# Transposing blocks by DMA in 16-bit halves instead of by TensorE, in a decoder layer

## The chip, the cores and the metric

The kernel runs on one core of a Trainium2 chip. TensorE (PE) multiplies matrices and writes PSUM; VectorE (DVE) and ScalarE (ACT) do elementwise work; GpSimd (POOL) does a little elementwise work and issues some DMAs; SyncE (SP) issues most DMAs. The metric is the device time of one launch in microseconds. The kernel before takes 2216.7 us (median of 3 runs, 2216.55 to 2218.02).

## The reference, cut to what matters

One decoder layer in float32 over 256 tokens of width 2048: a SwiGLU feed-forward, a mixer of two parallel branches (windowed attention and RWKV-7), a cross-attention into 256 memory tokens, a second SwiGLU, a final norm. The part around the change is the end of the mixer and the start of the cross-attention:

```python
merged = gate_attn * (y_attn @ w_proj_attn) + gate_rwkv * (y_rwkv @ w_proj_rwkv)
x = x + merged @ w_out
# cross-attention
h = rms_norm(x, norm_g)                  # the third norm
mn = rms_norm(mem, mem_norm_g)
q = (h @ w_q).reshape(B, T, CROSS_HEADS, CROSS_HEAD_DIM)
km, vm = jnp.split(mn @ w_kv, 2, axis=-1)
```

## The kernel before

**Products.** Every weight product runs on PE in a split form of float32. A weight tile of two 128-row chunks by 512 columns (512 KB, one *unit*) is loaded by SP into a tile `raw`. ACT casts it to `hi` (L370), DVE forms `lo = raw - hi` (L371), and PE does three matmuls for each chunk and each half of the tokens: hi·hi, lo·hi, hi·lo (L447 to L449). The left operand is the activation, turned so that features lie on the partitions, and split into hi and lo in the same way. A product with w_proj_rwkv has 4 units for a block of 512 columns, one with w_out 8. Units are prepared ahead of their use: `next_item` loads four units ahead and casts two ahead, with four `raw` buffers and three `hi` and three `lo` buffers.

**Background work.** Everything else is written as generators in named groups of an `Interleave`. After each half of a unit (six matmuls) `bg.tick()` takes one step of the first generators of each group (as many as the group's limit). `later_by(n, steps)` and `idle(n)` let n ticks go by. This gives the order in which the program is written. A planner then puts the instructions of each engine in an order by the times that it expects, so that work whose data is expected early may stand ahead of its written place; a tile's slot is given when it becomes free, and its first writer waits for the slot's last user. `tc.issue_after` pins an instruction behind another.

**The stage around the change.** After the RWKV branch (`yr`) is ready, four products with w_proj_rwkv give the four column blocks n of the merged branches: DVE multiplies by the gate (L1595), POOL adds the attention branch (L1596) into `m`, a tile of 128 partitions, 2 token halves and 512 columns. `merged(m, n)` waits four ticks, lets PE transpose the block in eight 128 x 128 pieces (`feat`, L639: two PSUM banks of four pieces), and `split` (L644, L645) writes the hi part (ACT) and the lo part (DVE) into `mt`. Four products with w_out follow, which read `mt`: two of a product's eight units for each block n. After each, DVE adds the residual block (L1618) into `x2`, and `n3.block` transposes that block in eight pieces on PE, multiplies by the gain into hi (ACT, L695) and lo (DVE, L696), and sums the squares (ACT, L707). `n3.x` is read two products later, by w_cross_q. Between them runs the first product with w_cross_kv, whose left side is the memory. The memory's blocks (`memory`, L1602 to L1609) arrive already turned (`memt`) and need no transposes; its gain products stand on the same lines L695 and L696 as `mehi` and `melo`.

**Buffers.** The mixer's larger temporaries are tiles named by `t4`, 4 KB on each partition, which share 23 slots (N4). In this stage `mt` holds eight, the memory's hi and lo eight, `x2` up to four, and `mem` with `memt` two for the block in work.

**Queues.** SP's queue carries the weight loads and the memory's loads; POOL's queue carries the residual's reloads (L1615) and those of the gates. A load waits on SP for its `raw` buffer, that is for the `lo` of the unit four before it.

Of the kernel before, what the change touches and what calls it, by code (L numbers as in the profile page):

```python
# [6 lines left out]

F32 = mybir.dt.float32
F32R = mybir.dt.float32r
AF = mybir.ActivationFunctionType  # L10
ALU = mybir.AluOpType
AX = mybir.AxisListType
# [3 lines left out]
P = 128  # L16
# [120 lines left out]
def decoder_layer(ctx: ExitStack, tc: tile.TileContext, a: dict, out: bass.AP):  # L137
    nc = tc.nc
    act, dve, pool, pe = nc.scalar, nc.vector, nc.gpsimd, nc.tensor
# [7 lines left out]
    bg = Interleave()  # L147
# [5 lines left out]
    bg.group("norm", 1)  # L153
    bg.group("mem", 1)
    bg.group("stage", 4)

    def f32(x):
        return x.bitcast(F32)
# [14 lines left out]
    def idle(n):  # L173
        for _ in range(n):
            yield

    def later_by(n, steps):
        yield from idle(n)
        yield from steps
# [19 lines left out]
    def mixer_constants(sp):  # L199
# [31 lines left out]
        for v in (bdones, bdmean):  # L231
            r = sp.tile([P, P], F32R, name="ones_r" + str(len(ones_r)))
            act.copy(r[:], v[:])
# [36 lines left out]
    for entry in weight_plan(a):  # L270
# [4 lines left out]
        w, k0, nk, c0, n = entry  # L275
# [5 lines left out]
        for k in range(k0, k0 + nk, 2 * KU):  # L281
            u = len(units)
            units += [(v, k + i, c, 512) for v, c in zip(w, c0) for i in (0, KU)]
            for i in range(2):
                q = (k - k0) // KU + i
# [79 lines left out]
    def split_unit(u, rows=slice(0, KU)):  # L365
        n, raw = units[u][3], raws[u]
        hi = wp.tile([P, KU, n], F32R, tag="hi", name="hi")
        lo = wp.tile([P, KU, n], F32R, tag="lo", name="lo")
        for s in (slice(0, 1), slice(1, 2)) if u < AHEAD else (rows,):
# [4 lines left out]
    def two_parts(v, e):  # L374
        sp = at["pool"]
        hi = sp.tile([P, KU, 512], F32R, tag="thi" + e, name="thi")
        lo = sp.tile([P, KU, 512], F32R, tag="tlo" + e, name="tlo")
        act.copy(hi[:], v[:])  # L378
# [46 lines left out]
    def product(x: Act, w, skew=False, bank=acc):  # L425

        pw, _, nk, _, n = plan[at["product"]]
        assert pw.tensor is w.tensor
        at["product"] += 1
        o = [bank() for _ in range(2)]  # L430
        skewed = range(nk - AHEAD * KU - KU, nk, KU) if skew else range(nk, nk)
        for k in range(0, nk - KU * len(skewed), KU):
            bg.until(lambda: all(k + i in x.done for i in range(KU)))
            u = next_item()
            for t in range(2):
                multiply(o[t][:, :n], x, u, k, t, nk)
                bg.tick()
        last = [(k, next_item()) for k in skewed]
        for t in range(2):
            for k, u in last:  # L440
                multiply(o[t][:, :n], x, u, k, t, nk)
        return o
# [16 lines left out]
    def combinations(sp, x: Act, seven, name, ready=lambda: True, early=True, n=0):  # L459
# [4 lines left out]
        n = n or sum(4 if q in seven else 2 for q in pairs)  # L464
        parts = [sp.tile([P, n, P], F32R, tag=name + e, name=name + e) for e in ("hi", "lo")]
        c = {"parts": parts, "at": {}, "done": False, "seven": seven, "early": early}
# [40 lines left out]
    def product_pair(x: Act, c, w, first, middle, out, onto=()):  # L507
# [12 lines left out]
        for to, there in onto:  # L520
            b[to] = rings[to]()
            act.activation(b[to][:], there, AF.Copy, scale=2.0)
            begun.add(to)
# [56 lines left out]
    def gate_and_up(sp, x: Act, c, r, w):  # L580
# [14 lines left out]
        def out(b, to):  # L595
            t = int(to in ("p4", "p5"))
            if to in ("p2", "p4"):
                dve.tensor_tensor(hb[:, t], b[to][:], u3[:] if t else hb[:, 0], ALU.add)
                act.activation(hb[:, t], hb[:, t], AF.Silu, scale=r[t])
            else:  # L600
# [7 lines left out]
    def down(h: Act, c, w, xs):  # L608
# [6 lines left out]
        def first(b):  # L615
            act.activation(x00, b["p1"][:], AF.Copy, scale=0.5)

# [14 lines left out]
    def feat(tok, cols):  # L632


        b = tr()
        for i, col in enumerate(cols):
            for t in range(2):
                o = (2 * i + t) * P
                pe.transpose(b[:, o : o + P], tok[:, t, col : col + P], ident[:])  # L639
        return b[:].rearrange("p (c t) -> p c t", c=2)  # L640

    def split(x: Act, c, n, src):

        act.copy(x.at(0, c, n), src)  # L644
        dve.tensor_tensor(x.at(1, c, n), src, f32(x.at(0, c, n)), ALU.subtract)  # L645
        x.done |= set(range(c, c + n))


    class Norm:
# [9 lines left out]
        def begin(self, turned):  # L659
# [13 lines left out]
            begun = dve.tensor_tensor(lo[:, 0], raw[:, 0], f32(hi[:, 0]), ALU.subtract)  # L673
            act.activation(x.at(0, 1), turned[:, 1], AF.Copy, scale=g[1])
            with tc.issue_after(begun.ins):
# [7 lines left out]
        def features(self, n, src=None, turned=None):  # L683
# [5 lines left out]
            for h, b in enumerate(banks):  # L689
                for j in range(2):  # L690
# [3 lines left out]
                    g = self.gain[:, c : c + 1]  # L694
                    self.last = act.activation(self.x.at(0, c), b[:, j, :], AF.Copy, scale=g)  # L695
                    dve.scalar_tensor_tensor(  # L696
# [6 lines left out]
        def squares(self, n, src):  # L703

            with tc.issue_after(self.last.ins):
                for t in range(2):
                    act.activation(  # L707
                        junk_t[:], src[:, t, :], AF.Square, accum_out=self.ss[:, t, n : n + 1]
                    )
# [94 lines left out]
    def blk(d, n):  # L804
        return d[:, n * 512 : (n + 1) * 512].rearrange("(t p) n -> p t n", p=P)
# [14 lines left out]
    with tc.tile_pool(name="f1", bufs=1, reuse_waits="tile") as sp:  # L820
# [8 lines left out]
        turned = f32(sp.tile([P, KD, T], F32R, tag="hlo", name="hlo")[:])  # L829
# [52 lines left out]
    with tc.tile_pool(name="mx", bufs=1, reuse_waits="tile") as sp:  # L882
# [3 lines left out]
        def t4(name, shape=(P, 4, T), dt=F32):  # L886
            return sp.tile(list(shape), dt, tag="t4", name=name, bufs=N4)
# [4 lines left out]
        def act_tiles(name, n):  # L892
            return Act(
                [t4(name + "hi", dt=F32R) for _ in range(n)],
                [t4(name + "lo", dt=F32R) for _ in range(n)], 4,
            )
# [6 lines left out]

        C4 = [0, P, 2 * P, 3 * P]

        def halves_of(v, hi, lo):
            act.copy(hi, v)
            dve.tensor_tensor(lo, v, f32(hi), ALU.subtract)
            return hi, lo
# [670 lines left out]
        mt = act_tiles("mt", 4)  # L1580

        def merged(m, n):
            yield from idle(4)
            banks = [feat(m, C4[q : q + 2]) for q in (0, 2)]
            for q, b in zip((0, 2), banks):
                split(mt, 4 * n + q, 2, b)
                yield

        for n in range(4):
            g, m = t4("gl", (P, 2, 512)), t4("ml", (P, 2, 512))  # L1590
            pool.dma_start(g[:], blk(grd, n))
            pool.dma_start(m[:], blk(md, n))
            pr = product(yr, W["w_proj_rwkv"])
            for t in range(2):
                dve.tensor_tensor(g[:, t, :], pr[t][:], g[:, t, :], ALU.mult)  # L1595
                pool.tensor_tensor(m[:, t, :], g[:, t, :], m[:, t, :], ALU.add)  # L1596
            bg.spawn("feat", merged(m, n))

        n3 = Norm(g_cross)
        nm_ = Norm(g_mem, act_tiles("me", 4))  # L1600
# [11 lines left out]
        for n in range(4):  # L1612
            s = t4("x2", (P, 2, 512))
            x2.append(s)
            pool.dma_start(s[:], blk(x1d, n))  # L1615
            po = product(mt, W["w_out"])
            for t in range(2):
                dve.tensor_tensor(s[:, t, :], po[t][:], s[:, t, :], ALU.add)  # L1618
            bg.spawn("feat", later_by(2, n3.block(n, s)))
            if n == 0:  # L1620
                bg.spawn("mem", memory())

# [72 lines left out]
    with tc.tile_pool(name="f2", bufs=1, reuse_waits="tile") as sp:  # L1695
# [51 lines left out]
        for t in range(2):  # L1747
            m, r = (stat.tile([P, 1], F32, tag=e, name=e) for e in ("ms", "rs"))
# [72 lines left out]
```

## Time and profile before

| what | value |
|---|---|
| median of the runs | 2216.7 us |
| the profiled execution | 2216.82 us, of which 2215.1 us are its span |
| PE busy | 2200.8 us, 99% of the span |
| DVE, ACT, POOL busy | 1802.6, 1275.5, 106.9 us |
| PE clock granted | 0.999 |
| from HBM | 440.49 MB read, 23.59 MB written |

Products with w_proj_rwkv run from about 1267 to 1314 us of the span, those with w_out from there to about 1405 us. The page gives busy times over the whole span, a strip of 40 slices, the DMA queues, the chain of waits that ended last, and groups of instructions by line. The trace also answers for single tiles, lines and windows of time.

### The profile page before, as it was taken

The numbers are of one execution on the slowest core, as the hardware profiler recorded it, in microseconds if no ns is written. First come the engines' busy times: TensorE is split into PE (matmuls) and PEld (weight loads), VectorE is DVE, ScalarE is ACT, GpSimd is POOL, SyncE is SP. The second block draws the span as 40 slices with busy tenths as digits, with TensorE's granted clock in tenths as the row PEclk, the third lists the DMA queues.
The fourth block names the chain that finished last, engine by engine and source line by source line (L and its number), as shares of the span: only waits on it lengthen the run. The fifth ranks groups of instructions, "written<-read, shape, count | busy, mean of one in ns | idle before, by whom it ended". The sixth has DMA issues, their size and how long they took to land.

```text
span 2215.1 us, 28167 instructions
## 1 busy us (share of the span) xinstructions
PE 2200.8 (99%) x10520; PEld 1816.7 (82%) x10520; DVE 1802.6 (81%) x2316; ACT 1275.5 (58%) x1677; POOL 106.9 (5%) x184
## 2 busy tenths in 40 slices
PE   9999999999999999999999999999999999999998
PEld 7888888888888878888888888888888888888886
DVE  7998888998989476877667666558999899998996
ACT  7555555555556477644544546556565565655654
POOL 0000000000000001000321030001000000000000
PEclk9999999999999999999999999999999999999999
DMA  8555555565556545677778687558665666666573
GB/s 306 194 206 192 206 195 203 195 204 193 197 192 211 174 132 164 212 225 215 224 220 290 206 272 269 185 165 275 221 221 189 207 233 208 217 205 210 200 244 136
DMA packets 198280, 466.02 MB, mean 210 GB/s; under 512 B 15520, under 2 KB 17920, under 8 KB 187136
## 3 DMA queue, kind: packets, MB, share of 16 engines
q1 hardware_dynamic: 188976, 438.08, 59.2%
q0 software_dynamic: 7648, 23.52, 3.5%
q10 hardware_dynamic: 1520, 2.63, 0.3%
q8 instruction: 82, 1.34, 0.3%
q14 instruction: 54, 0.44, 0.1%
HBM read 440.49 MB, written 23.59 MB: 210 GB/s over the span
## 4 chain that ended last, share of the span: by engine, by line
PE 93%; DVE 3%; DMA 2%; ACT 1%; issue 1%; SPq 0%; POOLq 0%; POOL 0%; DVEq 0%; ACTq 0%
PE acc L447 19%; PE acc L448 19%; PE acc L449 19%; PE mm L447 8%; PE mm L448 8%; PE mm L449 8%; PE tr L639 2%; PE tr L448 2%; PE tr L447 2%; PE tr L449 2%; DMA raw<-in_ffn_w_up_dram 1%; DVE lo L371 1%; PE mm L1441 1%; DVE tlo L379 1%; PE tr L1371 0%
## 5 line engine op out<-in xcount | busy, mean ns | idle before, releaser
L370 ACT CAST hi<-raw 128x1024 fp32r<-128x1024 f32 (+1 forms) x768 | 754.6, 993 | 671.8 <-PE acc L449 483.1
L371 DVE TENSOR_TENSOR lo<-raw,hi 128x1024 fp32r<-128x1024 f32 (+1 forms) x768 | 879.4, 1149 | 314.9 <-ACT hi L370 312.4
L447 PE MATMUL acc<-hi,xhi 128*128 128x512 f32 (+1 forms) x1134 | 445.4, 394 | 1.9 <-ACT hi L672 1.1
L448 PE MATMUL acc<-lo,xhi 128*128 128x512 f32 (+1 forms) x1134 | 440.0, 388 | 1.6 <-DVE lo L371 1.5
L449 PE MATMUL acc<-hi,xlo 128*128 128x512 f32 (+1 forms) x1134 | 439.5, 388 | 0.0
L447 PEld LDWEIGHTS acc<-hi,xhi 128*128 128x128 f32 x1134 | 212.9, 188 | 47.4 <-issue 3.2
L448 PEld LDWEIGHTS acc<-lo,xhi 128*128 128x128 f32 x1134 | 213.0, 188 | 44.4 <-DVE lo L371 3.1
L449 PEld LDWEIGHTS acc<-hi,xlo 128*128 128x128 f32 x1134 | 212.9, 188 | 43.4 <-issue 0.4
L378 ACT CAST thi<-raw 128x1024 fp32r<-128x1024 f32 x192 | 199.9, 1051 | 64.8 <-DVE raw L401 44.4
L379 DVE TENSOR_TENSOR tlo<-raw,thi 128x1024 fp32r<-128x1024 f32 x192 | 232.3, 1218 | 0.9 <-ACT thi L378 0.3
L447 PE MATMUL mm<-hi,xhi 128*128 128x512 f32 x402 | 156.6, 389 | 0.0
L448 PE MATMUL mm<-lo,xhi 128*128 128x512 f32 x402 | 156.5, 389 | 0.0
L449 PE MATMUL mm<-hi,xlo 128*128 128x512 f32 x402 | 156.4, 389 | 0.0
L448 PE MATMUL acc<-lo,hhi 128*128 128x512 f32 x372 | 145.3, 391 | 0.0
L449 PE MATMUL acc<-hi,hlo 128*128 128x512 f32 x372 | 145.3, 391 | 0.0
L447 PE MATMUL acc<-hi,hhi 128*128 128x512 f32 x372 | 145.0, 390 | 0.0
L447 PEld LDWEIGHTS mm<-hi,xhi 128*128 128x128 f32 x402 | 75.5, 188 | 16.2 <-ACT hi L370 0.5
L448 PEld LDWEIGHTS mm<-lo,xhi 128*128 128x128 f32 x402 | 75.5, 188 | 15.8
L449 PEld LDWEIGHTS mm<-hi,xlo 128*128 128x128 f32 x402 | 75.5, 188 | 15.6
L448 PEld LDWEIGHTS acc<-lo,hhi 128*128 128x128 f32 x372 | 69.8, 188 | 14.4
L447 PEld LDWEIGHTS acc<-hi,hhi 128*128 128x128 f32 x372 | 69.9, 188 | 14.3
L449 PEld LDWEIGHTS acc<-hi,hlo 128*128 128x128 f32 x372 | 69.9, 188 | 14.0
(441 smaller groups left out, 3527.4 us busy)
## 6 DMA issues: line engine op xcount, KB each, us to landing
raw<-in_ffn_w_down_dram SPq DMA_DIRECT2D x88, 1024.0 KB, 5.2
raw<-in_ffn_w_gate_dram SPq DMA_DIRECT2D x84, 1024.0 KB, 5.1
raw<-in_ffn_w_up_dram SPq DMA_DIRECT2D x78, 1024.0 KB, 5.8
raw<-in_w_in_dram SPq DMA_DIRECT2D x136, 512.0 KB, 3.8
raw<-in_w_out_dram SPq DMA_DIRECT2D x32, 512.0 KB, 4.8
raw<-sums SPq DMA_DIRECT2D x20, 512.0 KB, 6.3
raw<-in_w_proj_attn_dram SPq DMA_DIRECT2D x16, 512.0 KB, 4.3
raw<-in_w_proj_rwkv_dram SPq DMA_DIRECT2D x16, 512.0 KB, 6.0
```

The costliest lines, as they stand in the source:

```text
L370: at["hi"] = act.copy(hi[:, s], raw[:, s])
L371: at["lo"] = dve.tensor_tensor(lo[:, s], raw[:, s], f32(hi[:, s]), ALU.subtract)
L378: act.copy(hi[:], v[:])
L379: dve.tensor_tensor(lo[:], v[:], f32(hi[:]), ALU.subtract)
L447: pe.matmul(o, xh, hi, start=first, stop=False, **how)
L448: pe.matmul(o, xh, lo, start=False, stop=False, **how)
L449: pe.matmul(o, xl, hi, start=False, stop=last, **how)
L639: pe.transpose(b[:, o : o + P], tok[:, t, col : col + P], ident[:])
L1441: pe.matmul(vb[to, (o + k) * P : (o + k + 1) * P][:, r], lhs(k, e), v[:, k, r], start=v is u and k + e == 0, stop=True, **ek,)
```

## The change

Three of the four merged blocks and all four blocks of the third norm are no longer transposed by PE. A new generator `by_dma` takes a float32 block as uint16 halves. ACT copies the two halves of every word apart into `u` (two copies of 128 x 1024 halves). SP issues four DMAs with `transpose=True`, one for each half word e and token half t, each 128 x 512 of 2-byte elements (128 KB) from `u` to `v`. ACT writes the transposed halves back into whole words in `out` (four copies of 128 x 512 halves). The user then works from `out` in SBUF instead of from PSUM: `split` for the merged blocks, gain products and squares for the third norm. The fourth merged block (n = 3) stays on PE. The new group `turn` steps up to four such generators at once. Seven blocks go through it: 56 PE transposes go, and 14 + 28 ACT copies, 28 DMAs on SP's queue and 21 `t4` tiles come.

```diff
+    bg.group("turn", 4)
...
+        def by_dma(src, name, use):
+
+            u, v = t4(name + "u", (P, 2, 2, 512), U16), t4(name + "v", (P, 2, 2, 4, P), U16)
+            out = t4(name + "t")
+            halves = src[:].rearrange("p t n -> p (t n)").bitcast(U16)
+            halves = halves.rearrange("p (t n e) -> p e t n", t=2, e=2)
+            whole = out[:].rearrange("p c t -> p (c t)").bitcast(U16)
+            whole = whole.rearrange("p (c t k e) -> p e t c k", c=4, t=2, e=2)
+            for e in range(2):
+                act.copy(u[:, e], halves[:, e])
+                yield
+            for e in range(2):
+                for t in range(2):
+                    nc.sync.dma_start(v[:, e, t], u[:, e, t], transpose=True)
+                yield
+            yield from idle(3)
+            for t in range(2):
+                for e in range(2):
+                    act.copy(whole[:, e, t], v[:, e, t])
+                yield
+            yield from use(out)
...
         def merged(m, n):
+            if n < 3:
+
+                def use(turned):
+                    for q in (0, 2):
+                        split(mt, 4 * n + q, 2, turned[:, q : q + 2])
+                        yield
+
+                yield from later_by(3, by_dma(m, "mt", use))
+                return
             yield from idle(4)
             banks = [feat(m, C4[q : q + 2]) for q in (0, 2)]
...
-            bg.spawn("feat", merged(m, n))
+            bg.spawn("turn", merged(m, n))
...
-            bg.spawn("feat", later_by(2, n3.block(n, s)))
+            def third(turned, n=n, s=s):
+                yield from n3.features(n, None, turned)
+                yield from n3.squares(n, s)
+
+            bg.spawn("turn", later_by(2, by_dma(s, "x3", third)))
```

More of the change, by code (lines that the diff above doesn't have):

```diff
@@ L9 @@
 F32R = mybir.dt.float32r
+U16 = mybir.dt.uint16
 AF = mybir.ActivationFunctionType
```

## The prediction

> **What bounds the kernel now.** I read the page's busy times and chain first, then busy time by windows around the change, then PE, ACT and SP in order of time.
>
> ```profile
> PE 2200.8 (99%) x10520; PEld 1816.7 (82%) x10520; DVE 1802.6 (81%) x2316; ACT 1275.5 (58%) x1677; POOL 106.9 (5%) x184
> ...
> PE 93%; DVE 3%; DMA 2%; ACT 1%; issue 1%; SPq 0%; POOLq 0%; POOL 0%; DVEq 0%; ACTq 0%
> ```
>
> PE is busy for 99% of the span and carries 93% of the chain, so PE's work comes off the time one for one, as long as nothing starves it. The windows below (us; then busy time and instructions of PE, PE's weight load, DVE, ACT and POOL, the clock granted, the share of the DMA engines, GB/s) are two products with w_proj_rwkv, then two with w_out.
>
> ```profile
> 1278.90:1290.70 11.80, 11.80 (x58) 9.87 (x57) 7.59 (x10) 5.30 (x6) 3.92 (x4) 1.00 0.94 309
> ...
> 1302.50:1314.20 11.70, 11.70 (x57) 9.77 (x56) 7.66 (x9) 5.30 (x6) 4.20 (x3) 1.00 0.80 259
> ...
> 1338.50:1360.40 21.90, 21.90 (x101) 18.01 (x100) 16.24 (x25) 15.96 (x32) 0.72 (x1) 1.00 0.90 322
> 1360.40:1383.00 22.60, 22.60 (x105) 18.80 (x105) 13.13 (x17) 14.08 (x24) 0.71 (x1) 1.00 0.65 215
> ```
>
> PE fills each stretch. ACT is half idle in the first two, but at 15.96 of 21.90 us in the third, where the memory's blocks come in; there and in the first the DMA engines are at 0.90 and more. These two are the tight places.
>
> **What goes.** One block costs PE this (start, duration, engine, line):
>
> ```profile
> 1285.79 0.39 PE L449 MATMUL acc<-hi,yrlo 128*128 128x512 f32 x1
> 1286.02 1.03 PE L639 MATMUL tr<-ident,ml 128*128 128x128 f32 x8
> 1286.81 0.48 PE L447 MATMUL acc<-hi,yrhi 128*128 128x512 f32 x1
> 1287.12 0.40 PE L448 MATMUL acc<-lo,yrhi 128*128 128x512 f32 x1
> 1287.36 0.39 PE L449 MATMUL acc<-hi,yrlo 128*128 128x512 f32 x1
> ...
> 1290.08 0.39 PE L449 MATMUL acc<-hi,yrlo 128*128 128x512 f32 x1
> ```
>
> From 1287.36 to 1290.08 twelve matmuls pass, so the pace is 0.227 us each. From the L449 at 1285.79 to the one at 1287.36 are three matmuls and the eight transposes: 1.57 - 0.68 = 0.89 us for eight, 0.11 us each. A unit of twelve takes 2.72 us. Seven blocks go: 7 x 0.89 = 6.2 us. That is all there is to win, 0.28%; DVE and ACT keep their splits, gains and squares, read from SBUF instead of PSUM. The group rows show another duration:
>
> ```profile
> L639 PE MATMUL tr<-ident,x x96: 270/272/327, 679.1 to 1509.8; 128*128 128x128 f32 x96
> ...
> L639 PE MATMUL tr<-ident,ml x32: 270/272/273, 1286.0 to 1322.1; 128*128 128x128 f32 x32
> ```
>
> 272 ns is the length of one pipelined transpose; a sum of these would be 15.2 us, but the next starts 0.11 us later, so I take 6.2. The Trainium skill (TensorE: Matmul & The Clock Gate, Part 4: PE-mode transpose) gives about 275 ns in a kernel's context; this trace agrees as to the length, and by that rule as a cost the 56 would give back 15.4 us instead of 6.2, which the starts contradict.
>
> **What comes on ACT.** The nearest rows are casts of as many elements:
>
> ```profile
> L370 ACT CAST hi<-raw 128x1024 fp32r<-128x1024 f32 x52 | 54.6, 1052 | 56.0 <-PE acc L449 53.0 <-DMA raw<-in_w_proj_rwkv_dram 3.0
> ...
> L645 DVE TENSOR_TENSOR mtlo<-tr,mthi 128x512 fp32r<-128x512 f32 x8 | 5.2, 686 | 0.5 <-ACT mthi L644 0.2
> ...
> L644 ACT CAST mthi<-tr 128x512 fp32r<-128x512 f32 x8 | 4.3, 589 | 3.0 <-PE tr L639 3.0
> ...
> L1615 POOL DMA_DIRECT2D x<-x1d x4 | 2.9, 725 | 34.6 <-ACT junk L707 34.6
> ```
>
> A `u` copy has 1024 elements on each partition (1.05 us), a join copy 512 (0.59, as L644). A block adds 2 x 1.05 + 4 x 0.59 = 4.5 us, seven blocks 31 us. If 16-bit elements at a stride went at half rate it would be 9.0; at double rate, 2.2. I take 4.5, because the count of elements is the same. A merged product, 48 matmuls or 10.9 us without its transposes, then has 5.3 + 4.5 = 9.8 us of ACT: it fits, barely. In the third window it is 15.96 + 4.5 = 20.5 of 96 matmuls or 21.8 us.
>
> How much lateness of ACT does PE forgive? The trace has a case, where ACT waited for a DMA of the memory:
>
> ```profile
> 1326.51 1.05 ACT L370 CAST hi<-raw 128x1024 fp32r<-128x1024 f32 x1 [1.67 <-PE acc L449]
> 1331.18 1.71 ACT L695 ACTIVATE mehi<-memt,cols 128x256 fp32r<-128x256 f32 x4 [3.62 <-DMA memt<-in_mem_t_dram]
> 1332.79 1.99 ACT L370 CAST hi<-raw 128x1024 fp32r<-128x1024 f32 x2
> ...
> 1340.93 1.05 ACT L370 CAST hi<-raw 128x1024 fp32r<-128x1024 f32 x1 [1.87 <-PE acc L449]
> ```
>
> ```profile
> 1334.47 0.39 PE L447 MATMUL acc<-hi,mthi 128*128 128x512 f32 x1
> 1335.14 0.50 PE L448 MATMUL acc<-lo,mthi 128*128 128x512 f32 x1 [0.28 <-DVE lo L371]
> ```
>
> On pace the cast after 1326.51 starts at 1329.23; it started at 1332.79, 3.56 us late, after ACT had stood 3.62 us for the DMA. PE lost 0.67 - 0.23 = 0.44 us. So a cast may be 3.1 us late for nothing, and beyond that PE pays one for one.
>
> The joins are where this can return: ACT waits there for the transposes, and behind a join on ACT's queue stand the hi casts, for which DVE's lo and then PE wait. The planner puts a join where it expects the data; it was too early for the memory by 3.6 us.
>
> ```profile
> memt<-in_mem_t_dram SPq DMA_DIRECT2D x4, 512.0 KB, 7.5
> ```
>
> A transpose carries a quarter of that load's size, so I take half its price, 0.22 us, for each merged block (bounds 0 and 0.44), 0.7 us in all. For the four blocks of x, ACT has room at three (14.08 of 22.60 us in the fourth window, less in the later ones). At the first it has none: on pace the cast after 1340.93 starts at 1343.65, and
>
> ```profile
> 1344.46 0.82 ACT L695 ACTIVATE xhi<-tr,cols 128x256 fp32r<-128x256 f32 x2
> ...
> 1346.69 1.05 ACT L370 CAST hi<-raw 128x1024 fp32r<-128x1024 f32 x1
> ```
>
> it is 3.04 us late already. Before it the `u` copies put 2.1 us, and the four gain products, which move behind the join, take 2 x 0.82 = 1.65 away: 0.45 us to PE. The join's 2.4 us and the gains come after; I cost them at nothing there, because the memory's squares and gains, which are not needed before 1405 (below), can stand behind them. Without that cover up to 4.0 us more.
>
> **What comes on SP and the DMA engines.** No transposing DMA is in the trace. Four a block, 128 KB each, wait on SP for the `u` copies, and behind them wait the weight loads, for which ACT's casts wait.
>
> ```profile
> L324 SPq DMA_DIRECT2D raw<-in_w_out_dram x10: 367/368/368, 1363.2 to 1388.6; - x10
> ...
> DMA to landing us min/median/max: 3.5/4.4/5.6
> ```
>
> ```profile
> DMA to landing us min/median/max: 3.6/5.6/7.9
> ```
>
> ```profile
> L1262 SPq DMA_DIRECT2D dl<-ld x4: 339/618/1690, 943.5 to 946.3; - x4
> ...
> DMA to landing us min/median/max: 4.2/4.4/5.0
> ```
>
> A plain load holds SP for 0.37 us. The nearest row is L1262: also 128 KB, gathered in runs of 128 bytes, median 0.62 us on SP and at most 1.69, landing after 4.4. I take its median, and no wait for `u`: 4 x 0.62 = 2.5 us a block; the bounds are 4 x 0.37 and 4 x 1.69 = 6.8. What a load may be late:
>
> ```profile
> 1360.87 1.06 ACT L370 CAST hi<-raw 128x1024 fp32r<-128x1024 f32 x1 [1.67 <-PE acc L449]
> ```
>
> ```profile
> 1363.21 0.37 SPq L324 DMA_DIRECT2D raw<-in_w_out_dram  x1
> ```
>
> The load at 1363.21 is for the unit four after the cast at 1360.87, so its cast is due at 1360.87 + 4 x 2.72 = 1371.75. Less 4.4 us of landing it has 4.1 us to spare, 2.9 with the 5.6 us of the merged stage; with ACT's 3.1 that is 7.2 and 6.0 us. At 2.5 us SP's hold costs nothing; at 6.8 us the three merged blocks cost 0.8 each, 2.3 us. On the DMA engines a block's 0.52 MB take 1.7 us at the first window's 309 GB/s, 0.16 of 10.9 us on top of 0.94: loads fall 1.1 us further behind a product, which stays under the 6.0 with D. Without that cover it would be 1.1 us a block.
>
> Deadlines: the third merged block is the tightest.
>
> ```profile
> 1303.24 3.53 POOL L1596 TENSOR_TENSOR ml<-gl,ml 128x512 f32<-128x512 f32 x2 [6.85 <-DVE gl L1595]
> ```
>
> ```profile
> 1314.24 1.28 DVE L1595 TENSOR_TENSOR gl<-acc,gl 128x512 f32<-128x512 f32 x2
> ```
>
> It is ready at 1306.77; the product with w_out begins at 1314.2 and reads it four units later, at 1325.1: 18.3 us. Copies 3.2 (one cast between), issues 2.5, landing 4.4, joins 2.4, splits 1.9 (two of L644, the last lo of L645): 14.4, so 3.9 us are left. The last block of x has a whole product, 21.8 us, before it is read.
>
> Tiles: each block takes three `t4` slots of 23, and the pool is full: in the group row above L1615 stood 34.6 us on POOL for a slot.
>
> ```profile
> 1354.57 0.72 POOL L1615 DMA_DIRECT2D x<-x1d  x1 [34.62 <-ACT junk L707]
> ```
>
> ```profile
> 1405.68 1.28 DVE L1618 TENSOR_TENSOR x<-acc,x 128x512 f32<-128x512 f32 x2
> ```
>
> That load of x2 was issued at 1354.57 for an addition at 1405.68, where the product with the memory starts too. A prefetch that finds its slot later costs nothing while it is less than some 40 us later.
>
> **Sum.** 6.2 - 0.7 - 0.45 = 5.1 us (0.23%). The profiled execution took 2216.82 us (span 2215.1), 0.1 above the median: 2216.8 - 5.1 = 2211.7. I count 0.2%, 4.4 us, as what a measurement of this kernel tells from no change.
>
> **The rivals.**
>
> ACT gives the gain back in part. For it: 9.8 of 10.9 us leaves little room to catch up, and at the first x block the forgiven lateness is used up. If each merged block pays 0.44 and half of the 4.0 us comes, 6.2 - 1.3 - 0.45 - 2.0 = 2.4: 2214.4. Against it: the memory's work has 50 us to give way.
>
> ACT becomes the bound: half-rate copies. Three merged products need 5.3 + 9.0 = 14.3 us in 10.9, 10.2 us in all, the third window 25.0 in 21.8, 3.2 more: 2216.8 - 6.2 + 13.4 = 2224.0. Against it: no row of ACT shows such a rate; for it: none shows 16-bit elements.
>
> The transposes hold SP, so weights come late (this one ends slower). With a hold of D a block, the wait for `u` included, the cost is 3(D - 6.0) + 4(D - 7.2). It undoes 5.1 us at D = 7.4 and decides against the change from there; D = 10, 2.5 us a transpose, costs 23.2: 2234.9. For it: SP runs ahead of PE, so a transpose may stand long for its `u` copy.
>
> ```profile
> 1322.92 0.63 SPq L1605 DMA_DIRECT2D memt<-in_mem_t_dram  x1
> ```
>
> ```profile
> 1338.49 1.28 DVE L1618 TENSOR_TENSOR x<-acc,x 128x512 f32<-128x512 f32 x2
> ```
>
> the load at 1322.92 is written behind the product whose sums DVE adds at 1338.49. Against: the planner orders SP by expected times, and every issue row is below 1.7 us. The Trainium skill (VectorE: DVE Perf Modes, The three transpose paths) has 1309 ns for a 128 x 128 transpose by DMA against 390 on TensorE, and its rules for authors choose TensorE where PSUM will do, as it does here. By that figure a DMA of four squares takes 5.2 us, D is 21, and the net loss an estimated 95 us. No transposing row of this trace confirms or denies it; L1262 speaks against it, and I give that size 0.02 of this rival's chance.
>
> The slots come too late for the third merged block: beyond 3.9 us of waiting PE stops one for one; at 10 us, 2217.8.
>
> A PE transpose costs its length: 15.2 us, 2201.6; the starts deny it.
>
> **How the numbers follow.** Forecast 0.45; gain returned in part 0.22; ACT bound 0.11; SP held 0.17; slots 0.04; lengths 0.01. Faster by over 0.2%: 0.45 + 0.01 = 0.46. Within 0.2%: 0.22 + 0.04 = 0.26. Slower: 0.11 + 0.17 = 0.28. The range from 2210.0 to 2226.0 reaches from below the case with every wait hidden (2210.6) to past ACT bound, and leaves out SP held and the lengths, 0.18. The forecast's own is 2210.0 to 2213.0, with the bounds 0 and 1.3 + 0.45 of its waits.
>
> **What would show it.** The PE row of L639 loses 56; the products with w_out go from 22.6 us (the fourth window) to 21.8, and PE's waits in the stage stay under 1.5 us. SP's transposes would show near 0.6 us each, ACT's copies 1.05 and 0.59, ACT's waits for `v` under 3 us. It is wrong if casts wait for `raw` in these windows, if a transpose holds SP over 1.7 us, or if a `u` copy takes 2 us.

## The result and the profile after

The changed kernel takes 2228.11 us (median of 6 executions, 2225.82 to 2231.14), the kernel before 2216.62 us beside it: a ratio of 1.0050 with a 95% interval of 1.0039 to 1.0060. It is slower by 11.5 us, where 5.1 us less was forecast, and it lies 2.1 us above the range. The profiled execution took 2228.18 us (span 2226.5).

The page of the changed kernel, busy times and chain by engine:

```profile
PE 2200.5 (99%) x10464; PEld 1812.5 (81%) x10464; DVE 1802.6 (81%) x2316; ACT 1304.3 (59%) x1719; POOL 106.8 (5%) x184
...
PE 92%; DVE 3%; DMA 2%; issue 1%; ACT 1%; POOL 0%; SPq 0%; POOLq 0%; DVEq 0%; ACTq 0%
```

PE has lost the 56 transposes (10520 to 10464 instructions) and is busy for as long as before: it stood more, and part of its matmuls ran at a lower clock. Shares of the whole span don't show where. Below are windows from one product's first matmul to the next one's (columns as in the prediction), first of the kernel before, then of the changed one: the product with w_proj_rwkv, the one with w_out, the one with w_cross_kv.

```profile
1268.33:1314.53 46.20, 46.20 (x217) 38.53 (x216) 28.14 (x29) 20.69 (x23) 15.17 (x14) 1.00 0.86 275
1314.53:1405.97 91.44, 91.16 (x417) 75.25 (x416) 57.60 (x73) 54.67 (x90) 6.36 (x6) 1.00 0.73 248
1405.97:1428.63 22.66, 22.66 (x106) 18.85 (x105) 12.96 (x16) 12.21 (x17) 0.70 (x1) 1.00 0.61 189
```

```profile
1267.59:1322.59 55.00, 46.56 (x194) 37.03 (x193) 26.77 (x26) 30.34 (x37) 15.47 (x15) 0.94 0.91 242
1322.59:1418.56 95.97, 91.46 (x394) 73.46 (x392) 58.84 (x75) 69.61 (x113) 5.03 (x6) 0.98 0.85 257
1418.56:1440.42 21.86, 21.86 (x98) 17.87 (x96) 12.62 (x16) 16.22 (x23) 1.78 (x1) 1.00 0.76 219
```

The products with w_proj_rwkv, where the merged blocks are made, take 55.00 us instead of 46.20; those with w_out, where the blocks of x are made, 95.97 instead of 91.44. Only the third, quiet stage shows the gain of one block, 0.80 us. Both slow stages have PE idle (8.4 and 4.5 us) and a granted clock under 1.00. The sum is 12.5 us longer.

What PE, then ACT, waited for in these stages (us in total, times, longest):

```profile
PE acc L449 <- DVE gl L1628: 5.2, 1, 5.2
PE acc L449 <- DVE x L1651: 3.7, 3, 1.9
PE acc L450 <- DVE lo L373: 2.3, 3, 0.8
PE acc L449 <- ACT hi L372: 1.8, 1, 1.8
```

```profile
ACT mtt L926 <- DMA mtv<-mtu: 9.4, 3, 5.0
ACT hi L372 <- DMA raw<-in_w_out_dram: 8.2, 5, 3.9
ACT mtu L917 <- POOL ml L1629: 8.1, 3, 3.9
ACT x3t L926 <- DMA x3v<-x3u: 7.4, 7, 1.9
```

None of these four waits of ACT is in the kernel before. ACT now stands for landings at the joins, the copies that put the halves back into words (mtt, x3t), for POOL's sum at the `u` copies (mtu), and for weights. How one of them reaches PE shows in order of time on ACT, DVE and PE, at the end of a product:

```profile
1302.01 1.04 ACT L372 CAST hi<-raw 128x1024 fp32r<-128x1024 f32 x1
1306.44 2.00 ACT L926 COPY mtt<-mtv 128x512 uint16<-128x512 uint16 x3 [3.39 <-DMA mtv<-mtu]
1308.31 1.03 ACT L372 CAST hi<-raw 128x1024 fp32r<-128x1024 f32 x1
```

```profile
1309.37 1.23 DVE L373 TENSOR_TENSOR lo<-raw,hi 128x1024 fp32r<-128x1024 f32 x1 [5.06 <-ACT hi L372]
1310.52 1.28 DVE L1628 TENSOR_TENSOR gl<-acc,gl 128x512 f32<-128x512 f32 x2
```

```profile
1305.71 0.39 PE L451 MATMUL acc<-hi,yrlo 128*128 128x512 f32 x1
1311.25 0.79 PE L449 MATMUL acc<-hi,yrhi 128*128 128x512 f32 x1 [5.15 <-DVE gl L1628]
1311.85 0.63 PE L450 MATMUL acc<-lo,yrhi 128*128 128x512 f32 x1
```

ACT stands 3.39 us for a landing and then joins for 2.00; the hi cast behind it starts at 1308.31; DVE, which works in order too, stands 5.06 us for that cast; and behind DVE's lo waits gl, the sum that empties the PSUM bank of the product just finished. PE waits 5.15 us for the bank, not for a weight. After it PE's steps are long: 0.60 us between the last two starts. That is a lower clock (the last section).

The durations behind it: the transposes (shortest, median, longest in ns), then the groups of ACT's copies in these stages (busy time and mean ns of one, idle time before them and what ended it):

```profile
L921 SPq DMA_TRANSPOSE x3v<-x3u x16: 1188/1258/2040, 1350.2 to 1425.2; - x16
...
L921 SPq DMA_TRANSPOSE mtv<-mtu x12: 1197/1315/2421, 1283.3 to 1319.8; - x12
...
DMA to landing us min/median/max: 2.4/4.0/7.2
```

```profile
L926 ACT COPY x3t<-x3v 128x512 uint16<-128x512 uint16 x16 | 11.3, 769 | 7.4 <-DMA x3v<-x3u 7.4
L926 ACT COPY mtt<-mtv 128x512 uint16<-128x512 uint16 x12 | 8.1, 762 | 9.4 <-DMA mtv<-mtu 9.4
L917 ACT COPY x3u<-x 128x1024 uint16<-128x1024 uint16 x8 | 8.0, 1042 | 3.0 <-DVE x L1651 3.0
...
L917 ACT COPY mtu<-ml 128x1024 uint16<-128x1024 uint16 x6 | 6.2, 1044 | 8.1 <-POOL ml L1629 8.1
```

Issuing one transpose holds SP for 1.26 to 1.32 us, twice what I took from L1262 (0.62); a `u` copy takes the 1.05 us forecast, a join 0.77 instead of 0.59. The four groups are 33.6 us of busy time.

### The profile page after: what moved, and what is told of

Read it like the earlier page. It is cut to its first block, busy times and chain, and to the rows that moved or that the text cites. A ratio compares the mean times of both kernels' runs of the same rounds, so it can differ in the third digit from the quotient of the medians.

```text
span 2226.5 us, 28144 instructions
## 1 busy us (share of the span) xinstructions
PE 2200.5 (99%) x10464; PEld 1812.5 (81%) x10464; DVE 1802.6 (81%) x2316; ACT 1304.3 (59%) x1719; POOL 106.8 (5%) x184
## 4 chain that ended last, share of the span: by engine, by line
PE 92%; DVE 3%; DMA 2%; issue 1%; ACT 1%; POOL 0%; SPq 0%; POOLq 0%; DVEq 0%; ACTq 0%
PE acc L449 18%; PE acc L450 18%; PE acc L451 18%; PE mm L449 8%; PE mm L450 8%; PE mm L451 8%; PE tr L450 2%; PE tr L449 2%; PE tr L451 2%; PE tr L641 2%; PE mm L1465 1%; DVE lo L373 1%; DMA raw<-in_w_out_dram 1%; DMA raw<-in_ffn_w_up_dram 1%; DVE tlo L381 1%
```

## The experiments

Three theories stood. A: ACT, which works in order, stands at joins and `u` copies for data, and the hi casts behind it are late. S: the transposes hold SP, and the loads behind them are late. W: ACT's added work is too much by itself. Times are medians; each experiment ran beside the kernel before on the same chip (2215.73 to 2215.95). The changed kernel's 2228.1 was taken beside 2216.6, so a difference between it and an experiment is uncertain by some 0.8 us. The windows of all kernels, taken as above, in us:

| kernel | median | ratio to before, 95% | w_proj_rwkv | w_out | w_cross_kv |
|---|---|---|---|---|---|
| before | 2215.8 | | 46.20 | 91.44 | 22.66 |
| after | 2228.1 | 1.0039–1.0060 | 55.00 | 95.97 | 21.86 |
| plain DMA | 2221.8 | 1.0019–1.0038 | 55.45 | 88.11 | 21.76 |
| hold only | 2220.3 | 1.0011–1.0030 | 46.00 | 96.89 | 21.76 |
| no transfer | 2214.6 | 0.9985–1.0004 | 48.33 | 87.93 | 21.76 |
| no transfer, `u` pinned | 2209.5 | 0.9958–0.9981 | 43.52 | 87.94 | 21.76 |
| merged only | 2228.3 | 1.0037–1.0071 | 55.87 | 92.90 | 22.66 |
| x only | 2216.2 | 0.9991–1.0010 | 46.20 | 91.25 | 21.90 |
| x only, pinned | 2219.4 | 1.0007–1.0026 | 46.20 | 93.80 | 21.76 |
| pinned | 2217.9 | 1.0003–1.0022 | 43.56 | 98.62 | 21.76 |
| pinned, memory by POOL | 2217.1 | 0.9996–1.0015 | 43.54 | 94.35 | 21.76 |
| x only, pinned, memory by POOL | 2218.5 | 1.0003–1.0022 | 46.20 | 92.63 | 21.76 |
| before, memory by POOL | 2218.8 | 1.0003–1.0023 | 46.20 | 92.40 | 22.65 |
| pinned, last x | 2216.1 | 0.9993–1.0011 | 43.76 | 95.96 | 21.76 |
| pinned, longer pause | 2211.0 | 0.9968–0.9986 | 43.57 | 89.88 | 21.78 |
| pinned, last x, longer pause | 2218.8 | 1.0005–1.0023 | 43.57 | 94.99 | 21.76 |
| before, longer pause | 2218.1 | 1.0001–1.0019 | 46.20 | 93.45 | 22.65 |

The windows are of one profiled execution each, up to 2.2 us from the median of its kernel.

**No transfer.** The 28 DMAs are left out, with the tiles `v` that they fill, and the joins read `u`.

```
-                    nc.sync.dma_start(v[:, e, t], u[:, e, t], transpose=True)
...
-                    act.copy(whole[:, e, t], v[:, e, t])
+                    act.copy(whole[:, e, t], u[:, e, t].rearrange("p (c k) -> p c k", c=4))
```

> The 28 transposing DMAs are left out: the joins on ACT read u directly, so the blocks come out unturned; ACT's 42 copies and everything else stay. Theory A (ACT stands at the joins until the transposes land, and the hi casts stand behind it): the 9.4 and 7.4 us of ACT's waits for mtv and x3v go, and the time falls to 2211 to 2214 us. Theory S (the transposes hold SP 1.2 to 2.4 us each and the weights come late): the same fall, this run does not tell it from A. Theory W (the 33 us of added copies on ACT are themselves too much): the time stays above 2222 us.

2214.6 us, a little above what A and S both expected: 13.5 us come back with the DMAs gone, and all of ACT's added copies still there. The products with w_out take 87.93 us, the full gain. So W does not make the loss. In the first stage 4.8 us were still missing (48.33 - 43.53).

**Plain DMA.** Same tiles and queue, copied instead of transposed (blocks stay unturned).

```
-                    nc.sync.dma_start(v[:, e, t], u[:, e, t], transpose=True)
+                    nc.sync.dma_start(v[:, e, t], u[:, e, t].rearrange("p (c k) -> p c k", c=4))
```

> The DMAs stay, four of 128 KB a block, but copy without transposing, so the blocks come out unturned. Theory S: SP is held about 0.4 to 0.6 us for each instead of 1.3, the weights come in time, ACT's 8.2 us of waits for raw w_out go, and the time falls below 2217 us. Theory A: the joins wait for a landing of 3 us or more all the same, and the time stays above 2221 us.

2221.8 us, 6.3 less than with transposes. The rows of L921 here, and what ACT waited for:

```profile
L921 SPq DMA_DIRECT2D mtv<-mtu x12: 465/588/725, 1284.7 to 1319.5; - x12
```

```profile
ACT mtt L926 <- DMA mtv<-mtu: 9.1, 4, 4.6
```

The hold is less than half (0.59 instead of 1.32 us), and ACT stands at the merged joins as long as before (9.1 us). The stages part accordingly: w_out has its full gain (88.11), w_proj_rwkv none (55.45). So the first stage loses as much to a plain copy as to a transpose, and what w_out loses needs the transposes. Whether by their hold of SP or by a later landing this run does not tell: ACT's waits at the joins of x fall with the hold, from 7.4 us to 1.7.

**x only**, and **merged only**.

```
-            if n < 3:
+            if n < 0:
```

```
-            bg.spawn("turn", later_by(2, by_dma(s, "x3", third)))
+            bg.spawn("feat", later_by(2, n3.block(n, s)))
```

> All four merged blocks are back on PE, the third norm's four blocks go by DMA. In the changed kernel the products with w_proj_rwkv took 55.0 us against 46.2 before, those with w_out 96.0 against 91.4, the first with w_cross_kv 21.9 against 22.7. If the loss sits in the merged stage, and w_out only starts late and with a drained prefetch, this run has 46.2, about 90 and 21.9: 2214 us. If the blocks of x lose by themselves, w_out stays at 94 to 96 and the time is 2218 to 2221 us.

> Three of four merged blocks go by DMA, the blocks of x by PE as in the kernel before. With the x blocks alone the time was 2216.2 us against 2215.8 us before. If the two parts are independent, the merged blocks alone hold the loss: 2225 to 2228 us. If the loss of the w_out stage (96.0 us in the changed kernel against 91.3 us with x alone) comes from the x blocks meeting the late merged blocks, the stage of w_proj_rwkv stays near 55 us and the total falls to 2220 to 2223 us.

2216.2 us, between the two times expected, and 2228.3 us: the blocks of x come out even, and the merged blocks alone lose as much as all seven. The parts are not simply additive by stage (w_out takes 92.90 us with the merged blocks alone, late work included, and 95.97 with both), but the question where the loss starts is answered: in the merged blocks.

**Hold only.** The transposes are issued and land, and the joins read `u`, so nothing waits for a landing (blocks unturned).

```
-                    act.copy(whole[:, e, t], v[:, e, t])
+                    act.copy(whole[:, e, t], u[:, e, t].rearrange("p (c k) -> p c k", c=4))
```

> All 28 transposes stay on SP's queue and land in v, but the joins read u, so no join waits for a landing (the blocks of x and of the merged branches go on unturned: the transposition is left out of the computation). Theory A (ACT stands at the joins until the transposes land, and the hi casts behind them are late): the time falls to that of the run without transfers, 2214.6 us, within 2 us. Theory S (five to seven microseconds of SP a block, weights late behind them): the time stays between 2225 and 2228 us. A time between 2218 and 2224 us says that both take part, in that proportion.

2220.3 us, between the two: both take part. Against the changed kernel, the joins' waits were worth 7.9 us (2228.1 - 2220.3); against the run without transfers, the transposes on SP and on the DMA engines are worth 5.6 (2220.3 - 2214.6). These are sums over stages that move apart: taking the joins' waits away gave 9.0 us in w_proj_rwkv and nothing in w_out (96.89 against 95.97), and taking the transposes away gave 9.0 in w_out and cost 2.3 in w_proj_rwkv (48.33 against 46.00). What the transposes do in w_out, on SP, then ACT, DVE and PE:

```profile
1366.95 5.63 SPq L921 DMA_TRANSPOSE x3v<-x3u  x4
1372.68 1.05 SPq L326 DMA_DIRECT2D raw<-in_w_out_dram  x2
```

```profile
1377.37 1.05 ACT L372 CAST hi<-raw 128x1024 fp32r<-128x1024 f32 x1 [0.81 <-DMA raw<-in_w_out_dram]
...
1384.27 1.05 ACT L372 CAST hi<-raw 128x1024 fp32r<-128x1024 f32 x1 [1.67 <-DMA raw<-in_w_out_dram]
```

```profile
1389.25 1.28 DVE L1651 TENSOR_TENSOR x<-acc,x 128x512 f32<-128x512 f32 x2
```

```profile
1389.99 0.50 PE L449 MATMUL acc<-hi,mthi 128*128 128x512 f32 x1 [1.93 <-DVE x L1651]
```

SP issues no weight for 5.63 us, the casts wait for weights, and again it is the bank, emptied late by a DVE sum, for which PE stands. With the slow clock after it this place costs 4.5 of the 9.0 us. Another 4.0 are lost at the start of w_out, and there no weight is late. ACT first stood for POOL's sum at a `u` copy, then worked without a pause, and its late casts held up DVE and the bank:

```profile
1308.77 1.05 ACT L917 COPY mtu<-ml 128x1024 uint16<-128x1024 uint16 x1 [3.86 <-POOL ml L1629]
```

```profile
1319.10 0.76 PE L449 MATMUL acc<-hi,mthi 128*128 128x512 f32 x1 [1.99 <-DVE gl L1628]
```

That is the third cause, which the next run takes away.

**No transfer, `u` pinned.** As without transfers, and each `u` copy is put behind the newest hi cast in ACT's order.

```
+                with tc.issue_after(at["hi"].ins):
+                    act.copy(u[:, e], halves[:, e])
```

> As the run without transfers (28 transposes left out, blocks unturned), and each u copy stands behind the newest hi cast in ACT's order instead of wherever it came out. The run without transfers kept one PE gap of 2.2 us in the stage of w_proj_rwkv, which I put down to u copies that stood 8.3 us for POOL's ml add. If that is right the gap goes and the whole gain of PE shows: 2216 less 6.2 less some tenths, 2210 us (2209.0 to 2211.5). Theory W (33.6 us of ACT work added to these stages cost time by themselves): 2214 to 2215 us as without the pin.

2209.5 us, as theory A had it: another 5.1 us (2214.6 - 2209.5). In the run without transfers ACT had waited for POOL's ml like this:

```profile
ACT mtu L917 <- POOL ml L1626: 8.3, 2, 4.5
```

Now the 8.3 us are down to 0.2, and PE has no gap in the three stages:

```profile
1267.89:1311.41 43.52, 43.52 (x193) 36.04 (x192) 26.70 (x27) 31.69 (x39) 15.43 (x15) 1.00 0.88 285
1311.41:1399.35 87.94, 87.94 (x394) 72.90 (x393) 59.49 (x75) 68.08 (x112) 6.40 (x6) 1.00 0.78 261
1399.35:1421.11 21.76, 21.76 (x98) 18.02 (x97) 12.60 (x16) 16.04 (x23) 0.69 (x1) 1.00 0.64 200
```

This is the account: from the changed kernel's 2228.1, 7.9 us of waiting for landings, 5.6 of transposes on SP, 5.1 of `u` copies waiting for POOL: 18.6 us, which had eaten the 6.4 us by which this kernel beats the one before (2215.9) and 12.2 more. The steps add up because each is the difference to the run before it. The three were taken away in this order, the planner puts the instructions anew for each kernel, and the stages above show that the causes overlap; in another order the shares could differ.

**Pinned.** The changed kernel whole, with `u` copies and joins behind the newest hi cast.

> All seven blocks by DMA as in the changed kernel, but the u copies and the joins are pinned behind the newest hi cast at the place where they are written, so the planner can't put them ahead of casts. Theory A: ACT's waits for ml, mtv and x3v fall from 25 us to under 8, and the time falls to 2211 to 2216 us. Theory S: the transposes hold SP as before, the weights are late, and the time stays above 2222 us.

2217.9 us, between what A and S expected: 10.3 of the 12.3 us come back, and ACT's waits for ml, mtv and x3v are gone. The first stage has its full gain, 43.56 us, with the transposes in place: there neither their landing nor their hold of SP (median 1.29 us) costs anything once ACT's order is right. But w_out takes 98.62 us, with two PE gaps of 2.09 us. (Such a gap is counted from the time at which the next matmul was due at the pace of 0.227 us; the idle time in a row is about 0.17 us less.) Ahead of the first, ACT stood for the memory's transposed tile, whose load SP had issued behind the four transposes of a block of x (the expectations below say eight, a miscount), and then worked without a pause until 1362.9:

```profile
1352.09 0.91 ACT L697 ACTIVATE mehi<-memt,cols 128x256 fp32r<-128x256 f32 x2 [3.09 <-DMA memt<-in_mem_t_dram]
```

```profile
1362.03 0.79 PE L449 MATMUL acc<-hi,mthi 128*128 128x512 f32 x1 [1.94 <-DVE x L1653]
```

**x only, pinned**, **memory by POOL** (three kernels: all seven blocks, the blocks of x alone, and the kernel before as a control), **pinned, last x** (merged blocks and the last block of x). The question is whether that wait makes the gaps.

```
-                nc.sync.dma_start(turned[:], a["mem_t"][:, 4 * n : 4 * n + 4])
-                nc.sync.dma_start(s[:], blk(W["mem"], n))
+                pool.dma_start(turned[:], a["mem_t"][:, 4 * n : 4 * n + 4])
+                pool.dma_start(s[:], blk(W["mem"], n))
```

> Merged blocks go by PE as in the kernel before; the four blocks of x go by DMA with u copies and joins behind the newest hi cast. Theory A: nothing stands in ACT's order any more, so four blocks gain 4 times 0.89 us: 2212.2 us (2211.2 to 2213.5). Theory S (in the run with all copies pinned, SP issued the loads of memt behind eight transposes, and ACT stood 3.1 us for memt): the gain is lost there, 2215.5 to 2218 us, and the stage of w_out is not shorter than the 91.3 us that x blocks without pins took.

> All seven blocks by DMA, u copies and joins behind the newest hi cast, and the eight loads of the memory blocks (memt and mem) issued by POOL instead of SP, so that they no longer stand behind the transposes. Theory S at memt (the pinned kernel lost its gain in the stage of w_out, 98.6 us, because ACT stood 3.1 us for a memt that SP issued late): that stage falls to 88 to 90 us and the time to 2209.5 to 2212 us. If the weights behind the transposes are what is late, the stage stays at 96 to 99 us and the time at 2216 to 2219 us.

> Only the blocks of x by DMA, pinned, memory loads on POOL's queue. Theory S at memt: the two PE gaps of 2.1 us in the stage of w_out go and the four blocks give 4 times 0.89 us: 2212.2 us (2211.3 to 2213.5). If the weights of w_out behind the transposes are what is late: as with the loads on SP, 2218 to 2220 us.

> The kernel before, with the memory loads on POOL's queue and nothing else: what moving these loads is worth by itself. In the kernel before PE has no gap in that stage, so all theories say no change, 2215.9 us within 1 us.

> The three merged blocks and the last block of x by DMA, u copies and joins behind the newest hi cast; the first three blocks of x by PE as in the kernel before. In the kernel with all copies pinned the stage of w_proj_rwkv took 43.56 us (46.20 before) and w_cross_kv 21.76 us (22.66 before), and only the stage of w_out lost, where three blocks of x met the memory loads on SP. If that meeting is the cause, the gains stay and w_out takes its 91.4 us: 2215.8 less 2.64 less 0.90, 2212.2 us (2211.2 to 2213.2). If the weights of w_out that SP issued behind the merged blocks' transposes carry their lateness into the stage, w_out takes 93 us or more (92.9 us where the merged blocks alone went by DMA unpinned) and the time is 2213.5 to 2215.5 us.

Pinned, the blocks of x are slower (2219.4) than unpinned (2216.2), with two gaps of 2.1 us: the way theory S had it, and past its 2218. Moving the memory loads to POOL does not repair it: the two times, 2217.1 and 2218.5, are those expected if the weights are what is late, though the stages (94.35 and 92.63) are shorter than pinned with the loads on SP. The control shows why that says little: the moved loads alone cost the kernel before 3.1 us, where none was expected. In the control POOL issues six of the eight within 3.8 us (1321.27 to 1325.10); SP had spread the same six over 18.9 (1322.92 to 1341.79). ACT then hardly stands at memt, but 6.6 us for weights of w_out in the control, where it had not in the kernel before, and 12.3 in the kernel with all blocks:

```profile
ACT hi L372 <- DMA raw<-in_w_out_dram: 12.3, 6, 3.7
```

And the kernel that should have kept the gains of four blocks and avoided the meeting (pinned, last x) lost them in w_out as well, 95.96 us, while ACT stood 8.5 us at memt; its 2216.1 us lie above both expectations, and the stage is as the second had it (93 us or more). So transposes of x ahead of the memory load are not needed for the loss there; that those of the merged blocks carry their lateness into it stays possible.

**Longer pause.** The memory blocks pause 12 steps instead of 6 between their loads and the first use; in the pinned kernel, in that with the last block of x, and in the kernel before.

```
-                yield from idle(6)
+                yield from idle(12)
```

> All seven blocks by DMA, pinned; each memory block pauses 12 steps instead of 6 between its loads and its first use. If ACT's standing at memt (3.1 us once in the pinned kernel) makes the PE gaps in the stage of w_out, that stage falls from 98.6 to about 88.8 us and the time to 2209.5 to 2212 us. If it is the x transposes' hold of SP that makes the weights late, the gaps stay and the time is 2215 to 2218 us.

> Merged blocks and the last block of x by DMA, pinned; memory blocks pause 12 steps. ACT stood 8.5 us at memt in this kernel without the longer pause (5.6 in the kernel before). If that wait is the cause, the stage of w_out takes 91 us instead of 96.0 and the time is 2212.2 us (2211.2 to 2213.2). Otherwise it stays at 2215.5 to 2216.5 us.

> The kernel before with the longer pause alone. PE has only gaps of 0.44 and 0.49 us in the stage of w_out there, so at most 0.9 us can be had: 2215.0 to 2216.0 us by every theory. A larger gain would mean that the pause, not the transposes, makes the faster kernels fast.

The pinned kernel with the longer pause takes 2210.99 us (2209.56 to 2212.26), ratio 0.9977, interval 0.9968 to 0.9986, as expected: faster by 5.0 us than the kernel before (2216.0), with all seven blocks by DMA. Its windows:

```profile
1267.86:1311.43 43.57, 43.57 (x194) 35.96 (x193) 25.45 (x24) 28.55 (x34) 15.45 (x14) 1.00 1.00 290
1311.43:1401.31 89.88, 88.54 (x394) 72.75 (x393) 58.49 (x70) 67.23 (x106) 6.00 (x5) 1.00 0.93 278
1401.31:1423.09 21.78, 21.78 (x98) 18.02 (x97) 15.59 (x24) 20.41 (x34) 1.41 (x2) 1.00 0.92 255
```

ACT does not stand at memt at all here. The 1.9 us that w_out still loses against 87.94 follow other waits of ACT:

```profile
ACT hi L372 <- DMA raw<-in_w_out_dram: 9.1, 5, 3.5
```

The other two were no test, because the pause counts steps of the work between, not microseconds, and the wait was still there, as in the kernel with the last block of x:

```profile
ACT mehi L697 <- DMA memt<-in_mem_t_dram: 7.4, 2, 5.1
```

They got slower by 2.6 us (against the same kernel with the short pause) and 2.1 us. What stays open is the cause of the loss in w_out. In the pinned kernel the gain came when the wait at memt went, and all four kernels with a longer wait at memt than the 5.6 us of the kernel before lost there; but so did two with a shorter one (3.1 us pinned, 5.1 with x only, pinned), and the changed kernel and hold only lost there with none at all. No run removed that wait alone, and both moves of the memory's work that were tried in the kernel before cost it 2.1 and 3.1 us.

## Why the prediction was wrong, point by point

- **The gain on PE** was right. Seven blocks at 0.89 us were 6.2 us; with these waits gone the kernel gained 6.4 (2215.9 - 2209.5), and the merged stage took 43.52 us where 46.20 - 3 x 0.89 = 43.53. The length of the transposes (rival, 2201.6) is out.
- **ACT's work** was nearly right: `u` copies 1.05 us as forecast, joins 0.77 instead of 0.59, so 5.2 us a block instead of 4.5. It fits beside PE: with all of it in place and nothing to wait for, PE had no gap. The rival of half-rate copies is out. (That no row of ACT shows 16-bit elements was a misreading: the squares at L707 write 128 x 512 of them, in 0.63 us.) The term for the first block of x, 0.45 us, was nothing: w_out takes 87.94 us in that run, 3.5 under before: three blocks are 2.7, and the 0.8 us by which PE was late in this stage of the kernel before, 0.44 of them at one weight, went as well.
- **The price of the joins** is the term that failed first: 0.22 us a merged block, bounds 0 and 0.44, scaled from a wait of 3.62 us that had cost PE 0.44. ACT stood 4.98 and 3.39 us at two of them (9.4 in all), and taking the waits of all seven blocks away was worth 7.9 us, all of it in the merged stage. The step behind it, "a cast may be 3.1 us late for nothing, and beyond that PE pays one for one", was read off one place, in the middle of a product. At the end of a product DVE's sum, which frees the bank, stands behind the lo of that late cast. There a cast that was due at 1304.73, 2.72 us after the one at 1302.01, started at 1308.31: 3.6 us late, for which the step gives 0.5 us, and PE paid 5.15. The bounds should have come from how late a landing can be (7.2 us here), not from a quarter of a load's size: a transposed 128 KB lands after 4.0 us, a plain copy of it after 3.2 (medians), both far from a quarter of memt's 7.5.
- **The wait at the `u` copies** was the second: the sum has no term for it. I took "no wait for `u`" for SP, and asked only what waits for the `u` copies, not what they wait for on ACT: POOL's ml add, which comes when PE, DVE and POOL are through with the block. ACT stood 8.1 us there; taken away, 5.1 us.
- **SP's hold** was the third: 4 x 0.62 = 2.5 us a block, measured 5.0 to 6.9; a plain copy of the same tiles holds 0.59 us, as L1262 did, so it is the transposing that takes longer. I had given 6.8 as the upper bound and priced it at 2.3 us for the merged blocks, none for x; by the run without transfers it cost 5.6 in all, in part because gaps drew a slow clock after them. And it fell elsewhere: pinned, the merged stage lost nothing with the hold in place; w_out is the stage that gained when the transposes went.
- **The rivals.** "ACT gives the gain back in part" named the mechanism and a time of 2214.4, with a merged block at 0.44 us; the stage lost (55.00 - 43.52) / 3 = 3.8 us a block. "The transposes hold SP" was a real second part. Its D counts the wait for `u` in: SP stood 0.3 us ahead of the first block and 1.9 to 2.0 ahead of each other, which makes 5.9 to 8.8 us, 7.2 on average, just under the 7.4 from which it was to decide alone. Its formula, block by block, gives 4.4 us. I had made rivals of two things that add up.
- **The slots** were harmless, as forecast: POOL's last reload of x2 went out at 1383.31 instead of 1354.57, 28.7 us later where 40 were allowed, and 35 us ahead of the sum that reads it (1418.26); PE nowhere waited for `mt`. **The last block of x** gave its 0.8 to 0.9 us in the quiet stage in every kernel.
- **The rule that chose TensorE** was right for the change as made, and not by its figures. A transposing DMA here (four squares of 128 x 128, one half of the bits) holds SP for 1.3 us and lands after 4.0; PE turns four squares of whole numbers in 0.44. The Trainium skill (VectorE: DVE Perf Modes, The three transpose paths) has 1309 ns a square for DMA, which I had turned into 5.2 us a DMA and a hold of 21 us a block: the traces have 5.0 to 6.9. With ACT's order pinned and the memory's pause longer DMA won by 5.0 us (2216.0 - 2211.0).

## What to carry to other kernels

Before work is given to an engine that works in order, ask of each new instruction what it waits for, not only how long it takes: here 33.6 us of added ACT work were free, and its waits cost 13.0 us (7.9 and 5.1). Put such work behind the cast that the bottleneck needs next, try that order in the whole kernel (here it mended one stage and left the next one open), and follow the lateness through the other in-order engines to whatever frees the bottleneck's buffers. A forgiven lateness that is read off one place holds for that place; look for the place with the least.

## What the runs showed of the hardware

A PE gap of about two microseconds can cost nearly twice itself. In the run without transfers PE has one gap of 2.18 us up to 1304.80, and then this (windows of 2 us; the clock granted is the third number from the end):

```profile
1302.80:1304.80 2.00, 0.00 (x0) 0.00 (x0) 1.88 (x3) 1.03 (x2) 0.00 (x0) 0.99 0.67 234
1304.80:1306.80 2.00, 2.00 (x5) 1.61 (x6) 2.00 (x2) 0.00 (x0) 1.96 (x2) 0.50 0.59 198
1306.80:1308.80 2.00, 2.00 (x8) 1.58 (x7) 0.39 (x1) 0.44 (x1) 2.00 (x2) 0.65 0.38 123
1308.80:1310.80 2.00, 2.00 (x10) 1.66 (x9) 0.69 (x1) 2.00 (x4) 0.20 (x1) 1.00 0.82 247
```

From 1304.80 to about 1308.3 the clock is half, and a matmul step takes 0.43 us instead of 0.227: eight steps in 3.50 us instead of 1.82. The stage lost 48.33 - 43.52 = 4.8 us: 2.2 of gap, 1.7 of slow steps, and 0.9 of gaps under 0.3 us. In the traces of these stages gaps up to 1.90 us that stood alone were followed by a clock of 1.00 (1.64 in the kernel before with the memory by POOL, 1.90 with x only), gaps of 1.97 to 2.10 by half in five cases and by 1.00 in two (x only, pinned), and gaps of 2.16 us or more always by half. Where a gap of 1.03 us came about a microsecond behind the first, a first one of 1.92 was followed by 1.00 (the changed kernel) and one of 1.66 by half (plain DMA), so the length alone does not decide. The Trainium skill (TensorE: Matmul & The Clock Gate, Part 1: The HAM clock gate) has the drop to 4/8 after an idle window of about 3.4 us. The traces agree with the half, not with the gap that it takes: about 2 us were enough here.

On SP, a transposing DMA of 128 x 512 two-byte elements within SBUF held the queue for 1.26 to 1.32 us (median), a plain one of the same tiles for 0.59; they landed after 4.0 and 3.2 us (5.0 and 5.8 for the merged blocks, 3.3 and 2.5 for those of x). The Trainium skill (Advanced Engine Details and Errata, X-Bar Transpose (TRN2)) calls transposing DMAs as fast as regular ones; for the landing that is near, for the issue it was not.
